# More of the U part ahead of the dense loop, gathers opened later, gates on ScalarE: one change to a streaming-encoder block

## The chip, the cores and the metric

The kernel runs on one core of a Trainium2 chip. A core has five engines that run on their own queues: TensorE (PE, with its weight loads PEld), VectorE (DVE), ScalarE (ACT), GpSimd (POOL) and SyncE (SP, which here only issues DMAs). The metric is the device time of one execution in microseconds (us); smaller is better.

## The reference

One encoder layer on 1024 tokens of width 1024. Two kinds of attention (stick-breaking and mLSTM) are mixed by an output projection; then a PEER mixer picks, for every token, 8 heads x 16 experts out of 16,384 and adds their outputs. The PEER part, cut to what matters here:

```python
scores = einsum('bshpc,hpnc->bshpn', h @ w_q, sub_keys)       # two halves of 128 keys per head
top_s, top_i = top_k(scores, 16)                              # then the best 16 of 16 x 16 sums
gate = softmax(best_s)                                        # 128 (expert, gate) pairs per token
u = expert_u[idx]; act = gelu(einsum('td,tkd->tk', x, u))     # U part
y = einsum('tk,tkd->td', gate * act, expert_v[idx])           # V part
```

All is float32. The kernel splits an operand into a rounded high half and a low half (high = round(x), low = x - high) and multiplies three pairs of halves.

## The kernel before

The 1024 tokens are cut into a group of 512 and two of 256. The PEER mixer treats them in two ways.

**Gathers.** 448 tokens (`G`) fetch their experts' rows: for each of 3 full tiles of 128 tokens, and a half tile that is packed onto 128 partitions, an indirect DMA on GpSimd's queue fetches one row of U per token (`gu`, 512 KB), VectorE multiplies it with the token and sums (L920); after all experts of the tile, another set of indirect DMAs fetches rows of V (`gv`), which VectorE scales and adds into `gy` (L931). That makes 448 + 448 = 896 gathers, in one stream, with four buffers (`GU`). The pool `gp` holds those buffers.

**Dense.** The other 576 tokens (`ND`) multiply with all 16,384 experts, in 128 blocks of 128 experts. The U part of a block (`block`) loads 512 KB of U, splits it (`uh` on ScalarE, `ul` on VectorE), makes 48 matmuls `da` and a gelu on ScalarE into `dg`. The V part (`dense`, `dense_out`) multiplies `dg` with a table of gates `dw`, splits it and a block of V, and makes 48 matmuls: 24 (`yr`) stay in PSUM all the time, 24 (`dy`) are summed there over `GB` blocks, then copied by ScalarE to `dt` and added to `dy` by VectorE.

**Gate table.** `wbuild` turns the experts and gates of 128 tokens into the table `w_d` in DRAM. It works in units of four tokens, 144 in all. A unit makes two one-hot tables, `wo1` from the first key (L985) and `o2` from the second (L986), on VectorE, scales the first with the gates on GpSimd into `wm` (L988), multiplies them per token on TensorE (`wps`), and ScalarE copies the result into `wst` (L993). In two of eight units (`ACT_HOT`) ScalarE makes the scaled second table instead (L981, L982) and VectorE only `wm` (L978). 32 tokens fill a `wst`, which goes to DRAM in one store of 2 MB; there are 18.

**Order.** The program is written as generators that `weave` mixes by their weights; a scheduler then orders each engine's instructions by priority (`urgent` raises it) and by when operands and buffers are there. The rough course: projections and the first attention part; attention for the later tokens beside `route(0)` and `route(1)` (the top-k of the first two groups); `out_proj(2)` and the first builds; `route(2)` beside more builds, U parts ahead (`ahead`, blocks of the list `AHEAD`, results kept in `g_d`) and the first gathers; the last builds; the dense loop with the rest of the gathers. `N_A` says how many blocks ahead, `N_G` how many gathers are mixed into these last two stages before the loop.

## Time and profile before

| | us |
|---|---|
| median of 3 runs | 3553.79 |
| lowest, highest | 3552.81, 3560.16 |
| the profiled execution's own time | 3561.83 |
| span of the profiled execution, first to last instruction | 3560.1 |

The profile is one execution. Over the span PE is busy 3048.9 us (86%), DVE 2954.9 (83%), ACT 1505.4 (42%), POOL 2024.9 (57%); the mean granted TensorE clock is 0.914 of 2.4 GHz. Since the limits change along the span, it is read by stretches: in a table of stretches each row has the stretch's bounds and length, then for every engine its busy time and count of instructions, then the granted clock, the mean busy share of the 16 DMA engines, and GB/s. A busy PE is not PE at its peak, since matmuls overlap.

### The profile page before, as it was taken

Reading aid. Unit: us, or ns where it says so; the run is one execution under the profiler, and the core shown is the slowest. Engines: PE = TensorE matmul, PEld = TensorE weight load, DVE = VectorE, ACT = ScalarE, POOL = GpSimd, SP = SyncE. Lnnn points to the kernel's source line nnn. Section 1 sums busy time; section 2 is a strip of 40 time slices with the busy share of each in tenths; the row PEclk is TensorE's granted clock in tenths of the full one; section 3 lists DMA queues with packets and bytes.
Section 4 is the critical chain, followed back from the end, with each engine's and each line's share of the span. In section 5 each row is a group of like instructions: output and inputs, shape, how many; then the busy total and the mean of one; then the engine's idle time right before and its main releaser. Section 6 shows DMA issues by size and latency. Waiting matters only on the chain.

```text
span 3560.1 us, 53635 instructions
## 1 busy us (share of the span) xinstructions
PE 3048.9 (86%) x18453; PEld 2738.0 (77%) x18453; DVE 2954.9 (83%) x5535; ACT 1505.4 (42%) x3195; POOL 2024.9 (57%) x1769
## 2 busy tenths in 40 slices
PE   6899998888877477975969999999999999999980
PEld 4677675566655367865969999999999999999980
DVE  6687745599999999998878888788888888888886
ACT  4665567845754335422543333333333333333320
POOL 4544445455888786675654455445555555555555
PEclk8999998899977678987979999999999999999995
DMA  4234426422466676677779998898999999998987
GB/s 171 82 118 132 121 68 199 142 86 79 134 212 192 200 238 223 212 234 258 245 267 323 314 313 306 297 324 303 331 317 318 311 319 319 329 332 312 326 274 270
DMA packets 403378, 850.16 MB, mean 239 GB/s; under 512 B 39320, under 2 KB 225176, under 8 KB 400800
## 3 DMA queue, kind: packets, MB, share of 16 engines
q0 software_dynamic: 129024, 469.82, 38.5%
q1 hardware_dynamic: 264480, 370.61, 31.8%
q10 hardware_dynamic: 9600, 6.29, 0.6%
q8 instruction: 145, 2.38, 0.3%
q14 instruction: 129, 1.06, 0.1%
HBM read 775.35 MB, written 70.95 MB: 238 GB/s over the span
## 4 chain that ended last, share of the span: by engine, by line
DVE 28%; PE 22%; issue 17%; DMA 16%; POOL 10%; ACT 2%; SPq 0%; POOLq 0%; DVEq 0%; ACTq 0%
DMA gv<-in_V_dram,idx 8%; POOL gu L918 7%; DVE gy L931 4%; DVE gu L920 3%; POOL gv L929 3%; DMA gu<-in_U_dram,idx 2%; PE wps L992 2%; DMA vf<-in_V_dram 2%; PE da L129 2%; PE da L131 2%; PE da L130 2%; DVE wo L986 2%; DVE wo L985 2%; PE dy L130 1%; PE dy L131 1%
## 5 line engine op out<-in xcount | busy, mean ns | idle before, releaser
L929 POOL DMA_INDIRECT gv<-in_V_dram,idx x384 | 504.7, 1314 | 438.3 <-DVE gy L931 361.2
L918 POOL DMA_INDIRECT gu<-in_U_dram,idx x384 | 498.6, 1298 | 424.8 <-DVE gu L920 355.1
L931 DVE SCALAR_TENSOR_TENSOR gy<-gv,gA,gy 128x1024 f32<-128x1024 f32 x448 | 595.7, 1330 | 121.1 <-DMA gv<-in_V_dram,idx 114.5
L920 DVE SCALAR_TENSOR_TENSOR gu<-gu,gh 128x1024 f32<-128x1024 f32 x448 | 582.4, 1308 | 117.6 <-DMA gu<-in_U_dram,idx 111.8
L131 PE MATMUL da<-dah,ul 128*128 128x320 f32 x1024 | 326.5, 319 | 41.0 <-DVE ul L125 40.9
L129 PE MATMUL da<-dah,uh 128*128 128x320 f32 x1024 | 326.6, 319 | 17.8 <-ACT dg L946 8.7
L1075 ACT COPY dt<-dy 128x320 f32<-128x320 f32 x336 | 142.4, 426 | 467.9 <-PE dy L131 362.5
L992 PE MATMUL wps<-wm,wo 128*128 128x128 f32 x1152 | 278.8, 408 | 57.7 <-DVE wo L986 39.9
L130 PE MATMUL da<-dal,uh 128*128 128x320 f32 x1024 | 324.4, 317 | 0.0
L129 PE MATMUL dy<-dgh,vh 128*128 128x320 f32 x1024 | 317.1, 312 | 4.4 <-ACT dt L1075 4.2
L131 PE MATMUL dy<-dgh,vl 128*128 128x320 f32 x1024 | 318.3, 311 | 0.0
L130 PE MATMUL dy<-dgl,vh 128*128 128x320 f32 x1024 | 318.2, 311 | 0.0
L129 PE MATMUL yr<-dgh,vh 128*128 128x256 f32 x1024 | 286.5, 285 | 27.9 <-ACT dgh L121 24.9
L129 PE MATMUL da<-h2h,uh 128*128 128x256 f32 x1024 | 290.2, 283 | 12.8 <-ACT dg L946 12.8
L992 PEld LDWEIGHTS wps<-wm,wo 128*128 128x128 f32 x1152 | 239.3, 233 | 79.3 <-issue 31.8
L130 PE MATMUL yr<-dgl,vh 128*128 128x256 f32 x1024 | 290.5, 285 | 3.4 <-DVE dgl L125 3.4
L131 PE MATMUL yr<-dgh,vl 128*128 128x256 f32 x1024 | 290.0, 284 | 0.5 <-DVE vl L125 0.5
L130 PE MATMUL da<-h2l,uh 128*128 128x256 f32 x1024 | 289.0, 282 | 0.0
L131 PE MATMUL da<-h2h,ul 128*128 128x256 f32 x1024 | 288.1, 281 | 0.0
L131 PEld LDWEIGHTS da<-dah,ul 128*128 128x128 f32 x1024 | 199.6, 195 | 44.8 <-DVE ul L125 44.3
L129 PEld LDWEIGHTS yr<-dgh,vh 128*128 128x128 f32 x1024 | 194.4, 192 | 29.1 <-ACT dgh L121 25.8
L129 PEld LDWEIGHTS da<-dah,uh 128*128 128x128 f32 x1024 | 200.2, 195 | 19.6 <-ACT dg L946 9.1
(450 smaller groups left out, 9155.4 us busy)
## 6 DMA issues: line engine op xcount, KB each, us to landing
uf<-in_UT_dram SPq DMA_DIRECT2D x128, 512.0 KB
vf<-in_V_dram SPq DMA_DIRECT2D x128, 512.0 KB
w_d<-wst SPq DMA_DIRECT2D x18, 2048.0 KB
dw<-w_d SPq DMA_DIRECT2D x32, 1152.0 KB
wfwq<-in_w_q_dram SPq DMA_DIRECT2D x192, 128.0 KB
wada<-in_w_adaT_dram SPq DMA_DIRECT2D x64, 256.0 KB
wfwo<-in_w_out_dram SPq DMA_DIRECT2D x96, 128.0 KB
wada<-in_w_adaT_dram SPq DMA_DIRECT2D x16, 512.0 KB
```

The costliest lines, as they stand in the source:

```text
L129: mm(out, sh, mh, start=start, stop=False, skip_group_check=skip)
L130: mm(out, sh, ml, start=False, stop=False, skip_group_check=skip)
L131: mm(out, sl, mh, start=False, stop=stop, skip_group_check=skip)
L918: nc.gpsimd.indirect_dma_start(out=u, out_offset=None, in_=a["U"], in_offset=bass.IndirectOffsetOnAxis(ap=idx[:, k : k + 1], axis=0))
L920: nc.vector.scalar_tensor_tensor(out=u, in0=u, scalar=1.0, in1=h2, op0=ALU.mult, op1=ALU.mult, accum_out=A[:, k : k + 1])
L929: nc.gpsimd.indirect_dma_start(out=vv, out_offset=None, in_=a["V"], in_offset=bass.IndirectOffsetOnAxis(ap=idx[:, k : k + 1], axis=0))
L931: nc.vector.scalar_tensor_tensor(out=y, in0=vv, scalar=A[:, k : k + 1], in1=y, op0=ALU.mult, op1=ALU.add)
L985: nc.vector.tensor_tensor(out=o1, **hot1)
L986: nc.vector.tensor_tensor(out=o2, in0=self.iota.unsqueeze(1).to_broadcast([P, 4, P]), in1=i2g[:, 0, ts].unsqueeze(2).to_broadcast([P, 4, P ...
L992: nc.tensor.matmul(ps[:, t], o2[:, t], m[:, :, t], start=True, stop=True)
L1075: nc.scalar.copy(t, ps)
```

## The change

- `AHEAD` grows from 12 blocks to 34; `N_A` from (6, 6) to (12, 22). The first 12 use the old single-buffered pool, the others the dense loop's own pool `ua`. `N_G` goes from (64, 64) to (96, 96).
- The gather pool `gp` is opened behind the attention pools, beside `mxp`, instead of ahead of `route(1)`.
- The stage that holds the end of `route(1)` and `out_proj(2)` gives the raised priority to the projection alone.
- In `wbuild` four ScalarE activations with a per-token scale replace GpSimd's product; `m` is laid out per token; `ACT_HOT` keeps one unit of eight instead of two.
- `GB` is 4 instead of 3: `dy` is summed over four blocks in PSUM.
- The last of the 18 gate groups gets DRAM tiles of its own (`we_d`, three stores for blocks 0-3, 4-31, 32-127), and the table for the first four blocks is asked for ahead of that group's build (`w_first`).
- In the first part of the kernel low halves move from GpSimd to VectorE and high halves from VectorE to ScalarE; weights there are loaded and split in 2 pieces instead of 4. `mod_q` moves to another pool.

```diff
+LAST = ((0, BB), (BB, 32), (32, 128))
-ACT_HOT = 5 * [(3, 7)]
+ACT_HOT = 5 * [(7,)]
-GB = 3
+GB = 4
-N_A = (6, 6)
+N_A = (12, 22)
-AHEAD = [3, 4, 5, 6, 7, 9, 11, 13, 15, 17, 19, 21]
+AHEAD = [4, 5, 6, 7] + list(range(10, 128, 4))
-N_G = (64, 64)
+N_G = (96, 96)
...
-        for q in range(4):
-            ks = slice(2 * q, 2 * q + 2)
-            wf = w.tile([P, 2, 128], F32, tag="wf", name=f"wf{name}_{q}", bufs=3)
+        n, e = (4, "v") if w is self.wp else (2, "g")
+        for q in range(KB // n):
+            ks = slice(n * q, n * q + n)
+            wf = w.tile([P, n, 128], F32, tag="wf", name=f"wf{name}_{q}", bufs=3)
             self.nc.sync.dma_start(wf, src[:, ks])
-            self.split(wf, wh[:, ks], wl[:, ks], "s", "g")
+            self.split(wf, wh[:, ks], wl[:, ks], "s", e)
...
-        self.split(L, Lh, Ll, "s" if on else "v", "g")
+        self.split(L, Lh, Ll, "s", "g" if on else "v")
...
-            self.split(W, *parts, "v", "g")
+            self.split(W, *parts)
...
-            self.split(Pm[:, live], ph[:, live], pl[:, live], "s" if f else "v", "g")
+            self.split(Pm[:, live], ph[:, live], pl[:, live], "s", "g" if f else "v")
...
+            if i == NG - 1:
+                self.w_first = self.gates_of(0)
...
-                    nc.gpsimd.tensor_tensor(out=m, in0=o1, in1=i2g[:, 1, ts].unsqueeze(1).to_broadcast([P, P, 4]),
-                                            op=ALU.mult)
+                    m = wb.tile([P, 4, P], F32, tag="wm", name=f"wm_{nm}", bufs=4)
+                    for t in range(4):
+                        col = slice(ts.start + t, ts.start + t + 1)
+                        nc.scalar.activation(m[:, t], o1[:, :, t], AF.Copy, scale=i2g[:, 1, col])
+                    ms = [m[:, t] for t in range(4)]
...
-            nc.sync.dma_start(self.w_d[i], st)
+            if i < NG - 1:
+                nc.sync.dma_start(self.w_d[i], st)
+            else:
+                for (b0, b1), w in zip(LAST, self.we_d):
+                    nc.sync.dma_start(w, st[:, b0:b1])
...
-                wt = self.wr.tile([P, NG, BB, TB], F32, tag="dw", name=f"dw{b}", bufs=2)
-                nc.sync.dma_start(wt, self.w_d[:, :, b : b + BB].rearrange("g i b t -> i g b t"))
+                wt = self.gates_of(b) if b else self.w_first
+                b0, w = next((b0, w) for (b0, b1), w in zip(LAST, self.we_d) if b0 <= b < b1)
+                (nc.sync if b else nc.gpsimd).dma_start(wt[:, NG - 1], w[:, b - b0 : b - b0 + BB])
...
-                self.gp = enter(left("gp"))
-                gathers = self.gathers()
...
-            self.mxp = enter(left("mxp"))
+            self.mxp, self.gp = enter(left("mxp")), enter(left("gp"))
+            gathers = self.gathers()
...
-            run(woven((first(r), 10 * (24 - CUT[3])), (first(chain(upto(p), upto(p))), 95), (wbs(*W_T[0]), 1.8 * 32 * len(W_T[0]))))
+            run(woven((r, 10 * (24 - CUT[3])), (first(chain(upto(p), upto(p))), 95), (wbs(*W_T[0]), 1.8 * 32 * len(W_T[0]))))
...
-                for b in AHEAD:
-                    nc.sync.dma_start(self.g_d[b], self.block(b, ub, (1, 1)))
+                for x, b in enumerate(AHEAD):
+                    nc.sync.dma_start(self.g_d[b], self.block(b, ub, (1, 1)) if x < N_A[0] else self.block(b, ua))
```

The order of instructions shows the change at three places. In the names, the last number is a tile's own; the one ahead of it counts (`gu_0` is the first gathered row of a tile of tokens). The first place is VectorE where the first gather stands. Before, it is amid the attention of the last tokens (`L`, `dm`) and the norm of the second group (`h`, `dal`):

```order
L505 SCALAR_TENSOR_TENSOR L_768_4_10603<-zs_768_4_10602,L_768_4_10603 128x512
L307 SCALAR_TENSOR_TENSOR dal<-h_3_9856,mod,dah 128x256
L920 SCALAR_TENSOR_TENSOR gu_0_13081,gA_13080<-gu_0_13081,gh_3_13071 128x1024
L723 SCALAR_TENSOR_TENSOR h_4_9887<-h_4_9887,scol_141,rwyh_9763 128x256
L505 SCALAR_TENSOR_TENSOR L_768_3_10713<-zs_768_3_10712,L_768_3_10713 128x512
L920 SCALAR_TENSOR_TENSOR gu_1_13096,gA_13080<-gu_1_13096,gh_3_13071 128x1024
```

Now it is amid the builds of the first gate tile (`wo`) and the last top-k of `route(1)`:

```order
L993 TENSOR_TENSOR wo_0_3_2_12495<-iota,wi_0_12137 128x512
L992 TENSOR_TENSOR wo_0_3_3_12561<-iota_b,wi_0_12135 128x512
L924 SCALAR_TENSOR_TENSOR gu_0_13000,gA_12999<-gu_0_13000,gh_3_12990 128x1024
L993 TENSOR_TENSOR wo_0_3_3_12560<-iota,wi_0_12137 128x512
L815 MAX gate<-mr_6_0_11951 128x8
L924 SCALAR_TENSOR_TENSOR gu_1_13003,gA_12999<-gu_1_13003,gh_3_12990 128x1024
```

The stream of gathers thus begins behind the attention, where 21 one-hot tables are already made.

The second place is TensorE at the last build unit. Before, units follow one another and the V part (`yr`, `dy`) follows at once:

```order
L992 MATMUL wps_3_6_17047<-wm_3_6_17042,wo_4_3_6_17041 128x128 x4
L992 MATMUL wps_3_7_17067<-wm_3_7_17057,wo_4_3_7_17056 128x128 x4
L129 MATMUL yr_17082<-dgh_17155,vh_17148 128x256
L129 MATMUL yr_17083<-dgh_17155,vh_17148 128x256
L129 MATMUL yr_17084<-dgh_17155,vh_17148 128x256
```

Now the unit's matmuls stand between those of U blocks (`da`), of which 473 follow before the first of the V part:

```order
L1002 MATMUL wps_3_7_18766<-wm_3_7_18756,wo_4_3_7_18755 128x128 x2
L131 MATMUL da_0_17843<-dah,uh_17839 128x320
L132 MATMUL da_0_17843<-dal,uh_17839 128x320
L133 MATMUL da_0_17843<-dah,ul_17840 128x320
L1002 MATMUL wps_3_7_18766<-wm_3_7_18756,wo_4_3_7_18755 128x128
```

Between the last matmul of the routing and the first of the V part there are 1221 U matmuls now and 504 before; 36 blocks' U matmuls stand ahead of the V part instead of 16.

The third place is VectorE at the end of the dense loop (`dy<-dy,dt` are its last adds, `dx` the output of the dense tokens). Before, the last tile's V gathers have come to their 89th of 128:

```order
L931 SCALAR_TENSOR_TENSOR gy_32196<-gv_88_34328,gA_29025,gy_32196 128x1024
L1048 SCALAR_TENSOR_TENSOR dx_3_35295<-yr_17083,mod,dx_3_35295 128x256
L1076 TENSOR_TENSOR dy<-dy,dt_35246 128x320
L1076 TENSOR_TENSOR dy<-dy,dt_35259 128x320
L931 SCALAR_TENSOR_TENSOR gy_32196<-gv_89_34401,gA_29025,gy_32196 128x1024
```

Now that tile's U gathers have come to their 124th:

```order
L924 SCALAR_TENSOR_TENSOR gu_123_32170,gA_29183<-gu_123_32170,gh_2_29181 128x1024
L1069 SCALAR_TENSOR_TENSOR dx_3_35215<-dy,mod,dx_3_35215 128x320
L1097 TENSOR_TENSOR dy<-dy,dt_35145 128x320
L1097 TENSOR_TENSOR dy<-dy,dt_35164 128x320
L924 SCALAR_TENSOR_TENSOR gu_124_32173,gA_29183<-gu_124_32173,gh_2_29181 128x1024
```

Behind the last add stand 132 gathers instead of 40.

## Rows read from the trace of the kernel before

**Rows 1.** The page's first line.

```profile
span 3560.1 us, 53635 instructions
```

**Rows 2.** Table of stretches, all instructions: PE, PEld, DVE, ACT, POOL, clock, DMA.

```profile
0.00:560.00 560.00, 481.57 (x2002) 356.56 (x2002) 372.67 (x657) 337.70 (x692) 248.20 (x253) 0.93 0.39 118
560.00:1000.00 440.00, 391.61 (x1735) 282.81 (x1735) 353.62 (x1310) 289.51 (x741) 269.29 (x315) 0.92 0.42 126
1000.00:1214.00 214.00, 131.24 (x624) 97.93 (x624) 209.79 (x636) 82.64 (x208) 179.03 (x158) 0.76 0.69 216
1214.00:1600.00 386.00, 298.99 (x1622) 278.18 (x1622) 375.33 (x749) 161.19 (x395) 276.22 (x241) 0.82 0.66 220
1600.00:1852.00 252.00, 186.34 (x950) 173.51 (x950) 219.30 (x347) 100.84 (x225) 159.49 (x122) 0.84 0.73 253
1852.00:3468.00 1616.00, 1559.15 (x11520) 1548.97 (x11520) 1365.80 (x1791) 533.49 (x937) 846.05 (x647) 0.99 0.91 315
3468.00:3560.00 92.00, 0.00 (x0) 0.00 (x0) 58.39 (x53) 0.00 (x0) 46.61 (x37) 0.50 0.79 275
```

**Rows 3.** Stretches, tiles gu, gu, gv alone: DVE, POOL (x126: two per gather).

```profile
1000.00:1214.00 214.00, 96.04 (x126) 75.66 (x60) 0.76 0.69 216
1214.00:1600.00 386.00, 17.79 (x27) 19.55 (x16) 0.82 0.66 220
1214.00:1600.00 386.00, 103.90 (x64) 73.48 (x61) 0.82 0.66 220
```

**Rows 4.** Groups by line and shape: count | busy us, mean ns | idle before, its releasers.

```profile
L986 DVE TENSOR_TENSOR wo<-iota,wi 128x512 f32<-128x512 f32 x108 | 107.0, 1005 | 3.8 <-PE wps L992 3.8
L985 DVE TENSOR_TENSOR wo<-iota_b,wi 128x512 bf16<-128x512 bf16 x108 | 89.3, 844 | 0.0
L978 DVE TENSOR_TENSOR wm<-iota_b,wi 128x512 f32<-128x512 bf16 x36 | 35.3, 981 | 2.3 <-PE wps L992 2.1
L988 POOL TENSOR_TENSOR wm<-wo,wi 128x512 f32<-128x512 bf16 x108 | 134.7, 1257 | 57.7 <-PE wps L992 30.3 <-DVE wi L964 7.5 <-issue 6.0
L982 ACT ACTIVATE wo<-wo,wi,wi 128x128 f32<-128x128 f32 x144 | 62.2, 488 | 0.0
L981 ACT ACTIVATE wo<-iota,wi 128x128 f32<-128x128 f32 x144 | 47.2, 394 | 45.2 <-DVE wi L966 26.9 <-PE wps L992 18.3
L993 ACT COPY wst<-wps 128x512 f32<-128x512 f32 x144 | 83.0, 581 | 116.4 <-PE wps L992 114.0 <-issue 1.7
```

**Rows 5.** Timeline, from 1308 us: start, length, instruction [idle before it].

```profile
1308.18 3.22 DVE L986 TENSOR_TENSOR wo<-iota,wi 128x512 f32<-128x512 f32 x1
1308.80 2.04 POOL L988 TENSOR_TENSOR wm<-wo,wi 128x512 f32<-128x512 bf16 x2
1311.32 0.41 DVE L985 TENSOR_TENSOR wo<-iota_b,wi 128x512 bf16<-128x512 bf16 x1
...
1311.66 0.68 DVE L986 TENSOR_TENSOR wo<-iota,wi 128x512 f32<-128x512 f32 x1
```

**Rows 6.** Stretches: tile da alone (PE, PEld, ACT), then all instructions.

```profile
1600.00:1852.00 252.00, 77.65 (x432) 69.13 (x432) 6.92 (x17) 0.84 0.73 253
3000.00:3200.00 200.00, 196.94 (x1478) 195.97 (x1477) 171.34 (x273) 66.87 (x117) 106.13 (x84) 1.00 0.94 327
```

**Rows 7.** Groups by line and shape: the adds and copies of the dense loop.

```profile
L1076 DVE TENSOR_TENSOR dy<-dy,dt 128x320 f32<-128x320 f32 x336 | 160.0, 484 | 15.2 <-ACT dt L1075 13.2 <-issue 1.5
L1075 ACT COPY dt<-dy 128x320 f32<-128x320 f32 x336 | 142.4, 426 | 467.9 <-PE dy L131 362.5 <-DVE dy L1076 92.6 <-PE da L131 4.0
```

**Rows 8.** Groups by line and shape, POOL, 0 to 560 us.

```profile
L125 POOL TENSOR_TENSOR Wl<-W,Wh 128x512 fp32r<-128x512 f32 x16 | 22.7, 1418 | 10.0 <-DVE Wh L123 10.0
```

**Rows 9.** The end: stretches, tile gv alone (DVE, POOL); waits from 3468 us.

```profile
3490.20:3553.80 63.60, 41.14 (x32) 36.00 (x28) 0.50 0.81 273
3468.00:3553.80 85.80, 51.39 (x40) 46.61 (x37) 0.50 0.84 288
DVE gy L931 <- DMA gv<-in_V_dram,idx: 26.4, 28, 3.1
```

More of the change, by code (lines that the diff above doesn't have):

```diff
@@ L203, in consts @@
         self.mod = c.tile([P, 48], F32, name="mod")
-        self.mod_q = c.tile([P, 2, 48], F32, name="mod_q")
+        self.mod_q = e.tile([P, 2, 48], F32, name="mod_q")
         self.scol = e.tile([P, KB], F32, name="scol")
@@ L331, in keep @@
         if not f:
-            self.split(src, parts[0], parts[1], "s", "g")
+            self.split(src, parts[0], parts[1])
     def proj_sb(self, p):
@@ L371, in proj_v @@
             if not f:
-                self.split(t, v[0], v[1], "s", "g")
+                self.split(t, v[0], v[1])
             yield
@@ L973, in wbuild @@
                 o2 = wb.tile([P, 4, P], F32, tag="wo2", name=f"wo2_{nm}", bufs=4)
-                m = wb.tile([P, P, 4], F32, tag="wm", name=f"wm_{nm}", bufs=4)
                 hot1 = dict(in0=self.iota_b, in1=i1[:, ts].unsqueeze(1).to_broadcast([P, P, 4]), op=ALU.is_equal)
                 if q % 8 in ACT_HOT[T]:
+                    m = wb.tile([P, P, 4], F32, tag="wm", name=f"wm_{nm}", bufs=4)
                     nc.vector.tensor_tensor(out=m, **hot1)
+                    ms = [m[:, :, t] for t in range(4)]
                     for t in range(4):
@@ L987, in wbuild @@
                                             in1=i2g[:, 0, ts].unsqueeze(2).to_broadcast([P, 4, P]), op=ALU.is_equal)
-                    nc.gpsimd.tensor_tensor(out=m, in0=o1, in1=i2g[:, 1, ts].unsqueeze(1).to_broadcast([P, P, 4]),
-                                            op=ALU.mult)
+                    m = wb.tile([P, 4, P], F32, tag="wm", name=f"wm_{nm}", bufs=4)
[3 more added lines that the diff above has]
+                    ms = [m[:, t] for t in range(4)]
                 ps = pp.tile([P, 4, P], F32, tag=tags[q % 2], name=f"wps{nm}")
                 for t in range(4):
-                    nc.tensor.matmul(ps[:, t], o2[:, t], m[:, :, t], start=True, stop=True)
+                    nc.tensor.matmul(ps[:, t], o2[:, t], ms[t], start=True, stop=True)
                 nc.scalar.copy(st[:, :, 4 * q : 4 * q + 4], ps.rearrange("p t n -> p n t"))
                 yield 1.8
-            nc.sync.dma_start(self.w_d[i], st)
+            if i < NG - 1:
[3 more added lines that the diff above has]
+                    nc.sync.dma_start(w, st[:, b0:b1])
     def block(self, b, ua, bufs=(DG, 2)):
@@ L1014, in block, with gates_of @@
         return g
+    def gates_of(self, b):
+        wt = self.wr.tile([P, NG, BB, TB], F32, tag="dw", name=f"dw{b}", bufs=2)
+        self.nc.sync.dma_start(wt[:, 0 : NG - 1], self.w_d[:, :, b : b + BB].rearrange("g i b t -> i g b t"))
+        return wt
     def dense(self, ua, dn):
@@ L1093, in build @@
         self.g_d = tiles("g_d", max(AHEAD) + 1, [P, ND])
-        self.w_d = dr.tile([NG, P, NB, TB], F32, name="w_d")
+        self.w_d = dr.tile([NG - 1, P, NB, TB], F32, name="w_d")
+        self.we_d = [dr.tile([P, b1 - b0, TB], F32, name=f"we_d{b0}") for b0, b1 in LAST]
         self.pp = pool("ps", 2, space=bass.MemoryType.PSUM)
```

## The prediction

> **What bounds the kernel now.** The table of stretches [rows 2] cuts the span of 3560.1 us [rows 1] at places that can be found in the trace: the end of the first attention part (560), the first gather (about 1000), the first gate build (1214), the end of the last routing (1600), the first matmul of the V part (1852) and its last add (3468). To 1000 TensorE is busy 482 of 560 and 392 of 440. From 1000 to 1600 VectorE is: 210 of 214 and 375 of 386, TensorE only 131 and 299. From 1600 to 1852 both have holes (186 and 219 of 252). In the dense loop TensorE has 1559 of 1616, 11,520 matmuls. The last 92 us hold no matmul, only gathers, for whose landings VectorE waits [rows 9]. So three limits follow each other, and the end of the kernel is the end of the gather stream. An edit is worth what it does to the limit of its stretch.
>
> **The change part by part.** Times of the order of work are counts of rows of the two orders; durations are rows of the trace.
>
> *0 to 560.* 112 subtractions of weight halves leave GpSimd and become 56 twice as wide on VectorE; 88 low halves of keys, scores and products follow; 64 high halves go from VectorE to ScalarE. A 128x512 low half took 1.42 us on GpSimd [rows 8]; VectorE does a two-operand 128x512 in 0.68 when it is not held up [rows 5]. By that, VectorE gains about 144 instructions, some 88 us, loses 64 casts of the same widths (by estimate no dearer than the subtractions) and the hold-ups by GpSimd's tensor work, which was most of its 248 us: near even on an engine with 373 of 560. TensorE is the limit here, and its idle time, 78 us, is the most there is to win; the shorter chains of split, product, split give part of it. I take -8, between -40 and +10 (the next stretch has VectorE at 80% and TensorE at 89%, more than here, so a busier VectorE costs little).
>
> *1000 to 1214.* The gather pool now opens behind the attention, so the first gather stands behind the first builds in VectorE's order instead of amid the attention. All 63 gathers of this stretch leave it: VectorE 96.0 us [rows 3] out of 210. What then ends last? TensorE's 131 us, at a granted clock of 0.76; with the idle share of the stretch before (11%) that is 147 us, -67, and less if the clock rises to the 0.92 of that stretch. Between -60 and -96; I take -78, nearer to TensorE's limit. The projection set ahead of the routing changes the order within, and neither's amount.
>
> *1214 to 1600.* 80 build units stand here before and after. A unit was two one-hot products on VectorE, 1.005 and 0.844 us on average, and a gate product of 1.26 us on GpSimd [rows 4]. The timeline shows why the average is high: an L986 took 3.22 us with GpSimd's gate products inside it, and 0.68 without; an L985 took 0.41 [rows 5]. With the gates on ScalarE (4 x 0.394, the rows of 128x128 activations [rows 4]), 70 units cost VectorE 1.09 each and 10 cost 0.68, together 83 us; before, 60 x 1.85 plus 20 x 0.98 were 131. That is -48, and other instructions that the gate products held up give some more, -8. Against it stand 105 gathers instead of 77 [rows 3], 28 x 1.29 (41.14 for 32 where nothing holds them up [rows 9]) = +36, and 5 more U blocks' 128x1024 splits at the same 1.29, +6. That is -14; with what the fewer hold-ups give the gathers (1.62 each here, 103.90 for 64 [rows 3]) I take -20, from -45 to +15. GpSimd's gate products took 134.7 us in all, and the means exceed the free durations by 108 x (0.33 + 0.43) = 82 us.
>
> The Trainium skill, "SBUF — State Buffer", section "Who interferes with whom", says that a VectorE instruction with two inputs in SBUF and a GpSimd instruction that reads SBUF shut each other out for the whole instruction, and that ScalarE waits on no one. By that rule the whole 134.7 us would come back to VectorE; the row of averages bears out 82 of it, and I use the rows. By the rule the sum would be lower by about 50 us, if VectorE always had work.
>
> *1600 to 1852.* 64 units before and after, but TensorE's order has 1221 U matmuls between the routing's last and the V part's first, against 504: 717 more, at 0.140 us (1616 over 11,520 [rows 2]) 100 us. 186 + 100 = 286 us, and at the dense loop's share of 96.5% 297: +45. TensorE then is the limit. Its clock was 0.84 here and would be near the loop's 0.99 with its holes filled; that takes some 5 us off. I take +40, from +20 to +75. VectorE (219, less the hold-ups by 48 gate products, plus 13 splits and 9 gathers) stays below, and the blocks' stores and loads are some 7 MB on DMA engines that are at 0.73. ScalarE gains 504 x 0.394 = 199 us over the two build stretches, loses 72 x (0.394 + 0.488) = 64, and gains some 1.9 for each of 20 U blocks (two gelus of 0.41, 6.92 for 17 [rows 6], and a 128x1024 cast, by estimate twice the 0.58 of a 128x512 copy [rows 4]): 262 becomes some 435 of about 660. Cover enough, unless its waits grow (below).
>
> *The dense loop.* 36 blocks' U part lies ahead of it instead of 16, so 10,560 matmuls are left. At the loop's mean of 0.140 that is 1481 us, at that of its best 200 us, 200 over 1478 [rows 6], 1429. The gathers inside are fewer (580 against 645 in VectorE's order), and V in fours takes away 88 adds of 0.48 us and 88 copies of 0.43 [rows 7], about 80 us on engines that TensorE sometimes waits for. I take 0.138: 1457, so -159, between -125 and -187. The gates' last group in three stores, and its extra small loads, lie beside this.
>
> *The end.* In VectorE's order 132 gathers now stand behind the last add of the dense loop; before it was 40. The 40 took 85.8 us and the last 32 of them 63.6, 1.99 each [rows 9]. 92 more cost 92 x 1.99 = +183. With 1.9 each it is +175; at the pace inside the loop, 1616 over 645 = 2.5, +230.
>
> **The sum:** -8 - 78 - 20 + 40 - 159 + 183 = -42, so a span of 3518 and, with 1.7 us around it, 3520. The profiled execution took 3561.83, 8 us more than the median of 3553.79; I take 8 off: **3512 us**. Most of what TensorE gains it hands to a longer gather tail, because the gathers start some 140 us later and the loop around them shrinks.
>
> **Rivals.** *ScalarE paces the builds* (slower). A unit's four scalings stand in one queue with the copy of the unit before, which waits for TensorE. 4 x 0.394 + 0.58 is 2.2 us per unit, 144 units 311 us, beside U blocks. For it: ScalarE already waited 116 us in front of that copy [rows 4], and now each wait holds the next unit's gates too. Against it: 435 of 660 leaves room, and buffers are four deep. Price: 1214 to 1600 becomes +40 and 1600 to 1852 +75 instead of -20 and +40, 95 us more: 3607. It decides from 42 us on, that is when the two build stretches together last over 700 us instead of 658.
>
> *TensorE closes its holes* (faster). The loop runs at its best pace (-187) and the builds' end costs +20, since the clock rises; the tail at 1.9. 3512 - 28 - 20 - 8 = 3456. For it: the pace of 0.135 is seen over whole stretches; against it: DMA engines at 0.91 in the loop.
>
> *The terms cancel* (no change): a loop at its old mean (-135 instead of -159) and a tail at 2.1 each (+193 instead of +183) are enough: 3546. The change does do what it says: the order has 36 split U blocks ahead of the first gate product of the loop, against 18.
>
> **How the numbers follow.** The forecast, 3480 to 3546, 0.48; TensorE closing its holes, 0.18; no change, 0.11; ScalarE pacing, or a tail as slow as in the loop, 0.23. Faster by over 0.2% is 0.66, same 0.11, slower 0.23 (0.2% is about what a measurement of this kernel can tell from no change). The range takes in the ends of the large terms, tail and loop, and most of both outer cases: 3450 to 3600.
>
> **What would show it.** Right: the first gather near 1140; stretches with builds where L986 and L985 take 0.68 and 0.41 throughout; the first V matmul near 1785; its last add near 3245; then some 270 us without a matmul, at 2 us per gather. Wrong: ScalarE idle in front of the copy of a build unit while TensorE waits for a scaled gate; a first V matmul after 1830; a loop above 1480; a tail above 300 or below 250.

## The result, and the profile after

The changed kernel took 3511.37 us (median; 3502.86 to 3513.13) beside 3555.35 for the kernel before: ratio 0.987, interval 0.985 to 0.989, 44 us faster. The forecast was 3512.

The profiled execution's span stands against [rows 1]:

```profile
span 3511.4 us, 53484 instructions
```

The limits change at events, and the events moved, so the stretches are cut here at the events of each kernel: the first top-k of the routing, the first gate unit, the last top-k, the first V matmul, the last add into `dy`, the end. Columns as in [rows 2]: bounds, length, busy time of PE, PEld, DVE, ACT, POOL, clock, DMA share, GB/s. First after:

```profile
0.00:697.90 697.90, 614.30 (x2582) 448.80 (x2583) 446.53 (x882) 476.31 (x991) 119.90 (x155) 0.94 0.42 131
697.90:1120.20 422.30, 365.79 (x1805) 275.05 (x1803) 395.87 (x1669) 251.93 (x659) 260.76 (x305) 0.92 0.32 98
1120.20:1517.20 397.00, 288.55 (x1838) 271.33 (x1838) 362.59 (x895) 218.55 (x605) 258.97 (x217) 0.82 0.79 269
1517.20:1786.70 269.50, 223.87 (x1671) 220.55 (x1672) 203.89 (x324) 168.94 (x432) 102.30 (x81) 0.91 0.88 314
1786.70:3249.90 1463.20, 1420.02 (x10562) 1413.36 (x10560) 1223.79 (x1633) 463.24 (x784) 766.80 (x579) 0.99 0.92 319
3249.90:3511.00 261.10, 0.00 (x0) 0.00 (x0) 174.97 (x148) 0.31 (x1) 152.81 (x128) 0.50 0.82 274
```

The same table of the kernel before, at the same events:

```profile
0.00:709.60 709.60, 617.75 (x2581) 452.20 (x2582) 452.84 (x801) 455.68 (x983) 334.01 (x355) 0.93 0.42 129
709.60:1218.00 508.40, 389.56 (x1794) 288.00 (x1794) 487.23 (x1817) 256.32 (x659) 362.50 (x371) 0.85 0.50 152
1218.00:1617.00 399.00, 305.09 (x1663) 283.65 (x1661) 385.17 (x790) 163.26 (x398) 285.40 (x248) 0.82 0.66 221
1617.00:1853.50 236.50, 177.34 (x898) 165.14 (x898) 206.96 (x292) 97.33 (x221) 151.81 (x115) 0.84 0.72 252
1853.50:3468.30 1614.80, 1559.15 (x11520) 1548.97 (x11520) 1364.60 (x1787) 532.78 (x936) 844.85 (x647) 0.99 0.91 315
3468.30:3560.00 91.70, 0.00 (x0) 0.00 (x0) 58.09 (x53) 0.00 (x0) 46.31 (x37) 0.50 0.79 274
```

Row by row, after less before, with the forecast term in brackets: -12 (-8), -86 (-78), -2 (-20), +33 (+40), -152 (-159), +170 (+183). The sum is -49 (-42). (The forecast's stretches were cut at slightly other places, so a term and its row agree only to some us.) Three of the six rows are large, and they largely cancel: the last add comes 218 us earlier (3250 instead of 3468), and 170 of that is handed to a stretch without a matmul.

The units' instructions, groups by line (count, busy us, mean ns, idle before and its releaser), against [rows 4]; L992 and L993 are the one-hot products of L985 and L986, L998 the new scalings, L1003 the copy:

```profile
L993 DVE TENSOR_TENSOR wo<-iota,wi 128x512 f32<-128x512 f32 x126 | 89.8, 728 | 5.0 <-PE wps L1002 4.9
L992 DVE TENSOR_TENSOR wo<-iota_b,wi 128x512 bf16<-128x512 bf16 x126 | 61.0, 498 | 2.9 <-ACT wm L998 2.9
L998 ACT ACTIVATE wm<-wo,wi 128x128 f32<-128x128 bf16 x504 | 165.7, 406 | 51.5 <-DVE wo L992 50.8 <-DVE wi L968 0.7
L1003 ACT COPY wst<-wps 128x512 f32<-128x512 f32 x144 | 82.5, 576 | 18.4 <-PE wps L1002 18.1
```

VectorE's two products fell from 1.005 and 0.844 us to 0.73 and 0.50. ScalarE's wait in front of the copy fell from 116 us to 18, and the new scalings wait for VectorE (51 us) far more than VectorE waits for them (3 us).

The gate matmuls on TensorE changed too. No term of the forecast has this. They are two instructions per token; first before, then after:

```profile
L992 PE MATMUL wps<-wm,wo 128*128 128x128 f32 x1152 | 278.8, 408 | 57.7 <-DVE wo L986 39.9 <-DVE wm L978 10.8 <-POOL wm L988 3.5
L1002 PE MATMUL wps<-wm,wo 128*128 128x128 f32 x1152 | 186.0, 314 | 42.1 <-DVE wo L993 16.5 <-ACT wm L998 13.6 <-DVE wm L984 4.8
```

They keep TensorE busy 93 us less. It goes with the layout: the scalings write `wm` per token, so that a matmul reads neighbouring elements, where it read every fourth one before. The changed kernel shows both layouts side by side. From 1600 to 1717 us, at a granted clock of 1.00, it runs 360 instructions of this group. In the 48 that follow VectorE's six `wm` of that time (the units of `ACT_HOT`, still in the old layout) one took 0.38 to 0.40 us, as all took before; nearly all others took 0.28.

### The profile page after: what moved, and what is told of

It reads as the page before. It is cut to its first block, busy times and chain, and to the rows that moved or that the text cites. A ratio compares the mean times of both kernels' runs of the same rounds, so it can differ in the third digit from the quotient of the medians.

```text
span 3511.4 us, 53484 instructions
## 1 busy us (share of the span) xinstructions
PE 2912.5 (83%) x18453; PEld 2629.1 (75%) x18453; DVE 2807.7 (80%) x5545; ACT 1579.3 (45%) x3471; POOL 1661.5 (47%) x1462
## 4 chain that ended last, share of the span: by engine, by line
PE 26%; DMA 19%; issue 19%; DVE 18%; POOL 14%; ACT 3%; SPq 0%; POOLq 0%; DVEq 0%; ACTq 0%
DMA gv<-in_V_dram,idx 11%; POOL gu L922 9%; POOL gv L933 4%; DVE gy L935 3%; PE da L131 2%; PE da L133 2%; PE da L132 2%; DMA gu<-in_U_dram,idx 2%; PE wps L1002 2%; DMA gu<-in_U_dram,gix 1%; PE z L496 1%; DVE gu L924 1%; DMA vf<-in_V_dram 1%; DMA wada<-in_w_adaT_dram 1%; PE ipc L131 1%
## 5 line engine op out<-in xcount | busy, mean ns | idle before, releaser
L935 DVE SCALAR_TENSOR_TENSOR gy<-gv,gA,gy 128x1024 f32<-128x1024 f32 x448 | 583.3, 1302 | 168.9 <-DMA gv<-in_V_dram,idx 159.0
L933 POOL DMA_INDIRECT gv<-in_V_dram,idx x384 | 492.5, 1283 | 411.9 <-DVE gy L935 319.7
L924 DVE SCALAR_TENSOR_TENSOR gu<-gu,gh 128x1024 f32<-128x1024 f32 x448 | 555.2, 1249 | 148.3 <-DMA gu<-in_U_dram,idx 127.5
L1096 ACT COPY dt<-dy 128x320 f32<-128x320 f32 x248 | 105.7, 427 | 476.2 <-PE dy L133 399.4
L127 POOL TENSOR_TENSOR vlm<-kvrm,vhm 128x128 fp32r<-128x128 f32 x56 | 29.5, 528 | 451.6 <-ACT vhm L123 446.9
L1002 PE MATMUL wps<-wm,wo 128*128 128x128 f32 x1152 | 186.0, 314 | 42.1 <-DVE wo L993 16.5
L1002 PEld LDWEIGHTS wps<-wm,wo 128*128 128x128 f32 x1152 | 169.4, 216 | 49.1 <-ACT wm L998 31.5
```

The source lines that it names most:

```text
L127: e.tensor_sub(lo, src, hi.bitcast(F32))
L924: nc.vector.scalar_tensor_tensor(out=u, in0=u, scalar=1.0, in1=h2, op0=ALU.mult, op1=ALU.mult, accum_out=A[:, k : k + 1])
L933: nc.gpsimd.indirect_dma_start(out=vv, out_offset=None, in_=a["V"], in_offset=bass.IndirectOffsetOnAxis(ap=idx[:, k : k + 1], axis=0))
L935: nc.vector.scalar_tensor_tensor(out=y, in0=vv, scalar=A[:, k : k + 1], in1=y, op0=ALU.mult, op1=ALU.add)
L1002: nc.tensor.matmul(ps[:, t], o2[:, t], ms[t], start=True, stop=True)
L1096: nc.scalar.copy(t, ps)
```

## The experiments

Runs are numbered 1 to 12 in the order in which they stand here. Ratios are to the kernel before on the same chip, and their intervals are 95%. Runs 1 to 4, 5 to 7, 8 to 10 and 11 to 12 had a chip each, on which the kernel before took 3547 to 3556 us, so a difference of medians between these groups can be off by some 8 us. Lengths of stretches are those between the events above, each from one profiled execution.

**1. Which parts pay: the first four runs.** The gather pool early again:

```diff
-            self.mxp, self.gp = enter(left("mxp")), enter(left("gp"))
-            gathers = self.gathers()
+            self.mxp = enter(left("mxp"))
 ...
+                self.gp = enter(left("gp"))
+                gathers = self.gathers()
                 r = chain(self.early(xw), p, route(1))
```

> The changed kernel with the gather pool opened where it was before, ahead of the second half of the attention; all else as changed. In VectorE's order 63 gathers now stand ahead of the first gate build (0 in the changed kernel), and 67 behind the last add of the dense loop (132). Theory (each gather is paid once, at the pace of the place where it stands): the first gate build comes 80 to 98 us later (63 gathers at 1.53 us of VectorE), the tail gets 65 x 1.9 = 124 us shorter: 3511 + 88 - 124 = 3475 us. So the late opening would be a loss inside a winning change. Rival 1, the late opening is a gain of its own, since TensorE idles longer amid the gathers than VectorE works on them: the first build comes 98 us later, the tail is only 65 x 1.3 = 85 us shorter: 3524 or more. Rival 2, both are even: 3500 to 3511.

Measured: 3461.29 us, ratio 0.9746 (0.9715 to 0.9778). The table of stretches of this run, from the first top-k to the end:

```profile
700.90:1207.80 506.90, 386.09 (x1791) 285.75 (x1790) 488.12 (x1815) 254.99 (x658) 362.08 (x371) 0.85 0.50 152
1207.80:1600.50 392.70, 286.74 (x1854) 267.37 (x1852) 366.82 (x856) 223.15 (x610) 272.65 (x211) 0.85 0.78 263
1600.50:1882.70 282.20, 233.33 (x1743) 229.60 (x1744) 214.03 (x366) 173.48 (x440) 111.41 (x93) 0.91 0.90 323
1882.70:3324.00 1441.30, 1408.70 (x10489) 1403.73 (x10488) 1207.94 (x1545) 458.40 (x776) 750.29 (x568) 0.99 0.92 319
3324.00:3471.00 147.00, 0.00 (x0) 0.00 (x0) 98.01 (x86) 0.85 (x2) 74.56 (x66) 0.51 0.81 277
```

The first gate unit comes 88 us later, and the end without matmuls is 121 us shorter (148 against 269 from the last matmul, 63 gathers fewer). The stretches between make -6 together: the loop is shorter, the builds' end longer. So the theory holds (3475 us expected; this profiled execution took 3473, the longest of the four): a gather that stands early costs 88/63 = 1.4 us, one that is left for the end 121/63 = 1.9. The late opening looks like a gain of 86 us in the table after, and is a loss of some 1.3% in the kernel.

The gate product back on GpSimd (and `ACT_HOT` as before):

```diff
-                    for t in range(4):
-                        col = slice(ts.start + t, ts.start + t + 1)
-                        nc.scalar.activation(m[:, t], o1[:, :, t], AF.Copy, scale=i2g[:, 1, col])
+                    nc.gpsimd.tensor_tensor(out=m, in0=o1, in1=i2g[:, 1, ts].unsqueeze(1).to_broadcast([P, P, 4]),
+                                            op=ALU.mult)
```

> The changed kernel with the gate product back on GpSimd, and the quarter of the units with ScalarE's one-hot as before. 92 gathers stand ahead of the end of the last routing (105), 147 behind the last add (132). Theory (GpSimd's gate products hold VectorE's two-operand work up): VectorE's mean for the one-hot products goes back from 0.73 and 0.50 us to about 1.0 and 0.85; the stretch from the first build to the end of the routing gets 56 us longer less 13 x 1.29 for the gathers that left it, +39; the tail gets 15 x 1.9 = 28 us longer: 3511 + 67 = 3578 us. Rival, ScalarE paces the builds in the changed kernel as much as VectorE did before (the stretch is 397 us there against 399): the stretch keeps its length, 3511 + 28 - 17 = 3522 us.

Measured: 3586.95 us, ratio 1.012 (1.008 to 1.016), slower than the kernel before. Groups by line:

```profile
L996 POOL TENSOR_TENSOR wm<-wo,wi 128x512 f32<-128x512 bf16 x108 | 140.5, 1309 | 62.1 <-PE wps L1001 51.3 <-DVE gy L935 3.2 <-DVE wo L992 2.9
L993 DVE TENSOR_TENSOR wo<-iota,wi 128x512 f32<-128x512 f32 x108 | 106.7, 1002 | 13.1 <-PE wps L1001 13.1
L992 DVE TENSOR_TENSOR wo<-iota_b,wi 128x512 bf16<-128x512 bf16 x108 | 74.2, 703 | 4.7 <-POOL wm L996 4.7
```

With GpSimd's products the means of VectorE's two are 1.00 us, back where it was, and 0.70, between 0.50 and the 0.844 of before. The loss is 75 us by the medians (2.5% by the ratios), near the theory's 67, but it lies elsewhere. The stretch of builds and routing is 415 us (397), +18 where the theory had +39; the next is 312 (269), +43 where it had nothing; the loop is some 12 shorter, and the end behind the last matmul 297 (269), +28 as expected. The two middle stretches of this run, and its gate matmuls:

```profile
1115.70:1530.80 415.10, 327.76 (x1838) 305.14 (x1838) 400.87 (x874) 164.64 (x405) 322.11 (x264) 0.85 0.71 240
1530.80:1843.00 312.20, 271.46 (x1671) 259.67 (x1672) 234.72 (x297) 129.64 (x272) 171.09 (x126) 0.93 0.77 268
L1001 PE MATMUL wps<-wm,wo 128*128 128x128 f32 x1152 | 286.2, 405 | 39.3 <-DVE wo L993 20.9 <-POOL wm L996 10.3 <-DVE wm L984 6.1
```

VectorE is the limit of the first, at 401 of 415. In the second TensorE is: from 1600 us to its end it is busy 241 of 243 us, at a granted clock of 1.00. It runs the same 1671 matmuls there in 271 us instead of 224, and the gate matmuls alone, in their old layout again, take 52 us more. So the +43 are TensorE's, and the layout's. The edit takes back two things at once, GpSimd's rest and the layout. No run has one without the other. The rival, ScalarE as the pace, is out: its time fell, and the kernel got slower.

The list of 12 early blocks (`N_A` and `N_G` as before):

```diff
-AHEAD = [4, 5, 6, 7] + list(range(10, 128, 4))
+AHEAD = [3, 4, 5, 6, 7, 9, 11, 13, 15, 17, 19, 21]
```

> The changed kernel with the list of 12 blocks early, and the counts of before for how they and the gathers are woven; all else as changed. 76 gathers stand behind the last add (132). Theory (the loop's gain is handed to the tail): the loop gets some 22 blocks x 48 matmuls x 0.138 = 146 us longer, the stretch between the routing's end and the first V matmul some 33 to 40 us shorter, and the tail 56 x 1.9 = 106 us shorter: 3511 + 146 - 37 - 106 = 3514 us, the same within 10. Rival, the early blocks are the change's main gain (TensorE's holes at the builds' end get filled): the tail does not shrink by as much, 60 to 110 us slower, 3570 to 3620.

Measured: 3481.66 us, ratio 0.9817 (0.9795 to 0.9838), where the theory had 3514: faster than with 34 blocks, by 30 us in the medians, 40 in the profiled runs and 0.5% in the ratios. Its stretches from the first gate unit:

```profile
1114.00:1493.90 379.90, 259.93 (x1550) 237.69 (x1550) 346.79 (x880) 208.35 (x587) 251.88 (x211) 0.79 0.77 260
1493.90:1722.80 228.90, 138.51 (x998) 135.14 (x998) 173.65 (x283) 143.51 (x389) 93.17 (x69) 0.78 0.81 284
1722.80:3307.50 1584.70, 1551.20 (x11520) 1545.07 (x11520) 1333.27 (x1740) 502.64 (x845) 861.53 (x650) 0.99 0.92 320
3307.50:3471.00 163.50, 0.00 (x0) 0.00 (x0) 109.50 (x95) 0.85 (x2) 87.14 (x75) 0.51 0.82 279
```

The loop is 129 us longer than with 34, the builds' end 41 shorter, the tail 105 shorter (163.7 against 269 from the last matmul): +129 - 41 - 105 = -17. The theory's three terms were +146, -37 and -106. Another 17 us were in no theory: the stretch of builds and routing is 380 us instead of 397. VectorE is busy 16 us less in it; 8 of these are the splits of the six U blocks, and some 3 the five gathers, that no longer stand there. The first gate unit comes 6 us earlier besides. TensorE's holes are back (138.5 busy of 229) and nothing is lost by that.

The kernel before with ScalarE's gates and nothing else (their per-token layout and `ACT_HOT` with one unit of eight belong to them):

> The kernel before with nothing changed but the gate product: four scalings on ScalarE instead of one product on GpSimd, and one unit in eight with ScalarE's one-hot instead of two. 160 gathers stand ahead of the end of the last routing (141), 7 behind the last add (40). Theory: the stretch from the first build to the end of the routing gets 56 us shorter, less 19 more gathers at 1.29, so -31; the stretch behind it up to 10 us shorter; the tail 33 x 1.9 = 63 us shorter: 3554 - 31 - 63 - 5 = 3455 us, faster than the changed kernel. Rival, ScalarE paces the builds: the stretch stays at 399 us or grows, 3554 - 63 + 0 to 40: 3490 to 3530 us. Rival 2, the gathers inside the loop (654 against 645) and the missing tail make the loop itself longer, by 33 x 1.9: 3520.

Measured: 3441.16 us, ratio 0.9708 (0.9675 to 0.9741): more than twice the gain of the whole change, and 14 us below the theory. Three groups, and the stretches from the first gate unit:

```profile
L987 DVE TENSOR_TENSOR wo<-iota,wi 128x512 f32<-128x512 f32 x126 | 92.0, 746 | 1.7 <-PE wps L996 1.7
L986 DVE TENSOR_TENSOR wo<-iota_b,wi 128x512 bf16<-128x512 bf16 x126 | 55.1, 451 | 0.0
L996 PE MATMUL wps<-wm,wo 128*128 128x128 f32 x1152 | 184.2, 316 | 58.6 <-DVE wo L987 27.9 <-ACT wm L992 13.7 <-DVE wm L978 8.8
```

```profile
1210.30:1586.30 376.00, 267.39 (x1658) 248.80 (x1657) 346.27 (x840) 214.39 (x596) 261.45 (x208) 0.82 0.78 263
1586.30:1806.50 220.20, 138.21 (x903) 131.59 (x903) 179.76 (x328) 140.65 (x384) 99.20 (x82) 0.81 0.86 308
1806.50:3412.00 1605.50, 1556.75 (x11520) 1546.33 (x11520) 1364.59 (x1749) 529.76 (x935) 859.77 (x644) 0.99 0.92 315
3412.00:3441.00 29.00, 0.00 (x0) 0.00 (x0) 17.69 (x23) 0.67 (x2) 6.05 (x5) 0.56 0.78 278
```

Builds and routing 376 us instead of 399, the stretch behind 220 instead of 236, and 65 us less from the last matmul to the end (29 against 94, 8 gathers against 41); with 8 us ahead of the first unit and 7 in the loop, 119 in the profiled runs. In builds and routing VectorE, at 385 of 399 us before, is busy 346 although 21 more gathers stand in the stretch. VectorE's freed time was filled with gathers, and these are what shortened the end. TensorE's busy time fell as well, by the new layout (from 305 to 267 and from 177 to 138 in the two stretches); what that adds where VectorE is the limit was not separated.

**2. Both losses taken back, fours against threes, and the tail.** The pool early and 12 blocks early together:

> The changed kernel with both parts taken back that the last runs showed to cost time: the gather pool opened where it was before, and the list of 12 early blocks. What is left of the change is the gates on ScalarE, the splits of the attention that went from GpSimd to VectorE and ScalarE, the last projection ahead of the routing, and V in fours. 63 gathers stand ahead of the first build, 6 behind the last add. Theory (the two losses add up, and what is left beside the gates is worth some 10 us): 3461 - 30 + 6 for the tail that can't shrink below nothing = 3437 us, as the kernel before with ScalarE's gates alone (3441) or up to 15 us less. Rival, the splits and the projection are worth as much as the front showed in the changed kernel (10 us earlier at the first routing): 3410 to 3425. Rival 2, they cost: 3450 or more.

Measured: 3439.25 us, ratio 0.9695 (0.9659 to 0.9732). The two losses add up, and what is left beside ScalarE's gates is nothing that can be told from run 4. The projection ahead of the routing, one of these parts, was never run alone.

The same in threes:

```diff
-GB = 4
+GB = 3
```

> The run of both parts taken back, and V in threes as before. 88 adds of 0.48 us on VectorE and 88 copies of 0.43 on ScalarE come back into the dense loop. No tail of gathers is left to take it up (7 behind the last add). Theory (TensorE waits now and then for these engines, loop at 0.140 instead of 0.138 per matmul): 10 to 20 us slower than with fours. Rival, the loop is paced by the bytes that its DMA moves and fours change nothing: within 5 us.

Measured: 3471.07 us, ratio 0.9778 (0.9746 to 0.9809): 32 us slower by the medians, 0.8% of the kernel before, above the theory's 10 to 20. In the profiled executions it is 24 us, 14 of them from the first V matmul to the last (1623 against 1609).

Six gather buffers for the V gathers of the last tile (threes make the room):

```diff
+            if T == NH - 1 and k % 3 == 2:
+                vv = self.dn.tile([P, D], F32, tag="gx", name=f"gv{T}_{k}", bufs=2)
+            else:
+                vv = g.tile([P, D], F32, tag="gu", name=f"gv{T}_{k}", bufs=GU)
```

> The changed kernel with V in threes, which leaves room in the dense loop's pool for two more gather buffers, and with these two used by the V gathers of the last tile alone (every third of them), so that six gathers are in flight there instead of four. 129 gathers stand behind the last add (132). What is read is the pace of the tail: 1.9 us per gather in the changed kernel, with DMA engines at 0.84 and VectorE waiting 78 us for landings in 255 us. Theory (the tail is paced by what the DMA engines move): 1.75 to 1.9 per gather, tail 225 to 255 us. Rival, it is paced by the round trip through four buffers (GpSimd waits 64 us there for VectorE to give one back): 1.35 to 1.5 per gather, VectorE's own 1.3, tail 175 to 195 us, and the kernel some 70 us faster.

Measured: 3480.24 us, ratio 0.9797 (0.9759 to 0.9834), of two executions. Its partner is run 11 below, the same in threes with four buffers, 3534.82. The end without matmuls is 218 us instead of 270, for 131 and 132 gathers. What is waited for in this end, in run 11 (engine, what it waits for, us in total, times, longest):

```profile
DVE gy L935 <- DMA gv<-in_V_dram,idx: 82.0, 95, 2.4
POOL gv L933 <- DVE gy L935: 55.2, 55, 2.1
```

and with six buffers:

```profile
DVE gy L938 <- DMA gv<-in_V_dram,idx: 29.4, 53, 2.7
POOL gv L936 <- DVE gy L938: 4.1, 3, 1.7
```

A stretch of 200 us in this end, V gathers alone (DVE, POOL, clock, DMA share, GB/s), first of the changed kernel (run 11 issues 104 in the same 200 us too), then with six buffers:

```profile
3300.00:3500.00 200.00, 133.60 (x104) 123.90 (x104) 0.50 0.83 274
```

```profile
3270.00:3470.00 200.00, 163.15 (x127) 151.56 (x123) 0.50 0.94 342
```

GpSimd hardly waits any more for VectorE to give a buffer back, and the pace goes from 1.92 us per gather (200 over 104) to 1.57 (200 over 127), between the ranges of theory and rival. That the round trip through four buffers held the tail up is shown. What paces it at six is not: the DMA engines at 0.94 are the fullest (VectorE has 163 of 200 us, GpSimd 152), but no run has more buffers.

**3. What is left of the change.** The kernel before with ScalarE's gates and V in fours:

> The kernel before with the gates on ScalarE and, new here, V in fours (a small table of the modulation moves to a pool that closes early, to make room). Nothing else of the change is in it. 4 gathers stand behind the last add. Theory (fours are worth what the pair of runs in fours and threes showed, 0.8%, about 28 us, since the end of the dense loop is now the end of the kernel): 3441 - 28 = 3413 us. It would then be the fastest, and the other parts of the change (splits, projection, last group of gates in three stores) would cost some 25 us between them. Rival, fours only win back in the changed kernel what its extra loads cost there: 3430 to 3445 us.

Measured: 3447.76 us, ratio 0.9692 (0.9651 to 0.9734): no gain over run 4, where the theory had 28 us. The gates' last group stored whole again, on run 5:

> The run with both losses taken back (pool early, 12 early blocks, V in fours), and the gates' last group stored whole and loaded with the others as before: 31 small loads of 64 KB fewer in the dense loop. Theory (they lie beside other work, as the prediction had it): 3439 us, the same within 8. Rival, the small loads hold up the gate product of every fourth block (ScalarE's dgh split waits 248 us for it in the loop, and TensorE 32 us for that split): 15 to 25 us faster, 3414 to 3424.

Measured: 3434.02 us, ratio 0.9649 (0.9609 to 0.9689). The intervals of runs 5 and 9 overlap, and the loop has the same length (1610 and 1609 us), so the small loads don't hold it up. It is the fastest version of all, by its median, though not clear of run 5. The splits of the attention back on GpSimd, on run 5:

```diff
 ...
-            self.split(src, parts[0], parts[1])
+            self.split(src, parts[0], parts[1], "s", "g")
 ...
-            self.split(W, *parts)
+            self.split(W, *parts, "v", "g")
 ...
```

> The run with both losses taken back, and the splits of the attention's weights, keys, scores and products where they were before, on GpSimd, with the high halves as before. 3 gathers stand behind the last add (6). Theory (VectorE is far from full to 560 us and TensorE sets the end there; the first routing began 12 us earlier in the changed kernel): the first routing begins 8 to 12 us later, and the end with it: 3447 to 3451 us. Rival, the wider splits give TensorE nothing that lasts to the end, or cost by the work they put on VectorE to 1200 us: 3425 to 3439.

Measured: 3443.53 us, ratio 0.9684 (0.9639 to 0.9728). In the profile the first top-k comes at 702 us instead of 692, and the last add some 13 us later, as the theory had it; the medians differ by 4 us, inside their intervals. Over all profiles the first top-k comes at 702 to 710 us in the four kernels with the old splits and at 692 to 701 in the ten with the new ones. So the splits bring TensorE's first part forward by some 10 us, and what of that reaches the end can't be told.

The changed kernel in threes:

> The changed kernel with V in threes as before, nothing else. 130 gathers stand behind the last add (132). The two pairs so far disagree: fours were worth 28 us where the pool was early and 12 blocks were early, and nothing on the kernel before with ScalarE's gates. Theory (as the prediction had it, loop at 0.140 instead of 0.1385 per matmul): the loop gets 10,560 x 0.0015 = 16 us longer, 2 gathers fewer are left for the tail, the end comes 12 us later: 3523. Rival, ScalarE's dt copies that TensorE waits for (5 us in the loop) are all that fours touch: within 5 us of 3511. Rival 2, as in the pair that showed it: 3536 or more.

Measured: 3534.82 us, ratio 0.9967 (0.9944 to 0.999). In the changed kernel fours are worth 1.0%. The loop of this run, and what TensorE waits for in it:

```profile
1789.40:3264.40 1475.00, 1417.82 (x10489) 1407.74 (x10487) 1245.51 (x1702) 491.01 (x865) 755.47 (x573) 0.99 0.91 314
```

```profile
PE yr L131 <- ACT dgh L123: 28.9, 20, 5.5
PE yr L132 <- DVE dgl L127: 17.4, 10, 4.3
```

In the changed kernel these two are 1.8 and 2.7 us, and the wait for the U part's gelu is 25.4:

```profile
PE da L131 <- ACT dg L950: 25.4, 16, 4.5
PE yr L132 <- DVE dgl L127: 2.7, 3, 1.9
PE yr L131 <- ACT dgh L123: 1.8, 1, 1.8
```

From the first V matmul to the last it is 19 us longer (1475 against 1456), although 72 U matmuls fewer stand in it: 0.1406 us per matmul instead of 0.1379, or 28 us at the same count, where the theory had 16. It begins 3 us later, and the tail does not get shorter by what the loop gets longer. That makes the 23 us of the medians, near rival 2 and not the theory. Why fours bring nothing on the kernel before with ScalarE's gates (run 8) stays open: there TensorE waits as long in fours as in threes (74 and 72 us in the loop), and the loop is as long (1609 and 1605 us).

20 blocks early instead of 12, on run 9:

> The run with the pool early, the gates whole, V in fours, and 20 blocks early instead of 12. 38 gathers stand behind the last add (10). Theory (with 12 there is hardly a tail left, so the end is set by the stream of gathers and loads; a block early adds 0.59 MB of store and load, 8 of them 4.7 MB, 15 us at 316 GB/s, and gives only TensorE something): loop 8 x 48 x 0.14 = 54 us shorter, builds' end 10 to 20 longer, tail 28 x 1.9 = 53 longer: 3434 + 15 = 3449 us. Rival, the 80 us in which TensorE is idle between the routing's end and the first V matmul are filled by them at no cost: 3400 to 3420 us.

Measured: 3447.18 us, ratio 0.9704 (0.9674 to 0.9734). The stretches from the last top-k, with the first one of run 9 ahead of them:

```profile
1570.00:1788.80 218.80, 134.51 (x998) 130.38 (x998) 182.05 (x327) 142.08 (x388) 94.20 (x80) 0.81 0.86 313
1581.70:1807.60 225.90, 169.62 (x1286) 167.22 (x1287) 185.27 (x328) 151.96 (x406) 96.21 (x77) 0.87 0.89 318
1807.60:3358.00 1550.40, 1502.63 (x11136) 1495.19 (x11136) 1288.95 (x1632) 488.70 (x823) 836.73 (x617) 0.99 0.92 317
3358.00:3445.00 87.00, 0.00 (x0) 0.00 (x0) 57.69 (x54) 0.43 (x1) 40.78 (x36) 0.53 0.82 282
```

TensorE's holes fill from 135 us busy of 219 to 170 of 226 and the loop gets 60 us shorter; the end behind the last matmul grows from 39 to 87, and the stretch of builds and routing by 14. No gain, as the theory had it. Whether it is the 0.59 MB per early block or VectorE's order of gathers that takes it away was not separated: by the page 34 early blocks move 13 MB more than 12 (the second line is run 3's):

```profile
DMA packets 402337, 863.13 MB, mean 246 GB/s; under 512 B 39672, under 2 KB 211192, under 8 KB 399760
```

```profile
DMA packets 395999, 850.13 MB, mean 245 GB/s; under 512 B 38968, under 2 KB 210488, under 8 KB 393424
```

At the loop's 319 GB/s that is 41 us, and the spans differ by 40. It fits, but no run moved the bytes alone.

## Why the prediction was right

*0 to the first routing*, -8: measured -12, and run 10 gives 10 of it to the splits. TensorE's idle time was the right place to look.

*To the first build*, -78: measured -86. The 63 gathers left, and the clock in the stretch rose from 0.85 to 0.92. That TensorE would be the limit there did not come out: VectorE is still the busier engine, 396 of 422 against 366. The value held because it was taken between the two bounds. The term is right as a stretch. The prediction did not set it against its own price in the tail; that was in its rows (63 x 1.53 of VectorE there, 63 x 1.99 at the end), and would have told that this part loses.

*Builds and routing*, -20: measured -2, the term with the largest miss. The hold-up by GpSimd was right in kind: VectorE's means rise with GpSimd's products (run 2) and fall without them (run 4). In the two one-hot products its size was 0.277 + 0.346 us per unit, 67 us over 108, where the forecast said 82; GpSimd's weight splits (`wlwq`, `wlwo`) still run beside the builds. VectorE's busy time did fall by what the forecast had added up, from 385 to 363 us. What failed is the step from there to the stretch, which was to shrink by as much. VectorE's idle time grew from 14 to 34 us. Waits for gathered rows to land are 17 of these 34 and were 8 before. Runs 3 and 4, with fewer U blocks in the stretch, leave VectorE as idle (33 and 30 us) but less busy (347 and 346). Why it waits more was not separated.

The rule of the Trainium skill quoted there ("SBUF — State Buffer", "Who interferes with whom"), by which all of GpSimd's 134.7 us would come back to VectorE, was too much for these two products by half: 67 us came back in them in the changed kernel and 70 in run 4. What VectorE's other instructions got back is not in that count. That ScalarE waits on no one fits the scalings' 0.41 us, beside 0.39 for ScalarE's like-sized activations.

*Builds' end*, +40: measured +33, by luck. The forecast added 100 us to TensorE's busy time and left it 3.5% idle. Its busy time rose by only 47 us (177 to 224), since the gate matmuls took 77 us there instead of 123 beside some 770 more U matmuls; and it is idle for 46 of the 269.5 us, 31 of them in one wait for the last top-k's result. The layout's gain and that wait, both missing from the forecast, offset each other. The clock rose to 0.91, not near 0.99; from 1600 us on, TensorE is the limit, as the forecast had it (117 of 117 us to 1717, at a granted clock of 1.00).

*Dense loop*, -159: measured -152. From first to last matmul it is 1456/10,560 = 0.1379 us (0.138). Without fours it is 1475/10,488 = 0.1406 in the changed kernel (run 11). Fours alone do not make this pace: runs 5 and 9 have them and more gathers in the loop, and show 0.140.

*Tail*, +183: measured +170, for 132 gathers as counted, at 1.92 us in its middle.

*The 8 us* that were taken off for the profiled execution of before: the last median of before is 3555.35, 6.5 below that execution, so most of this holds. But the profiled execution of the changed kernel is only 1.8 above its own median.

The mechanism was right where the large terms are: TensorE's gain in the loop, the gathers that leave the stretch ahead of the first build, and the tail they lengthen, each within 13 us. That the sum came out within 1 us of the median is luck: the six rows miss their terms by -4, -8, +18, -7, +7 and -13, the span by -7, and the 8 us taken off make up for it. The statement that TensorE's gain is handed to the tail is shown by run 3: the loop's 129 us and the tail's 105 go and come together. The rival that ScalarE paces the builds is refuted by runs 2 and 4. The signs came nearly as named: the two products at 0.73 and 0.50 us (0.68 and 0.41), the first gather at 1143 us, the first V matmul at 1787, the last add at 3250, then 269 us without a matmul. The sentence that fell short is the one that was missing: the change was summed by stretches, never by its parts. By parts it is ScalarE's gates (-3%), fours (-1% in this kernel), against the late pool (+1.3%) and 22 more early blocks (+0.5%). These do not add up to the -1.3% of the whole, since fours bring nothing on ScalarE's gates alone (run 8).

## What to carry to other kernels

Where a stream of transfers ends the kernel, price each part of a change to the end of that stream: work that is moved away from an early stretch comes back behind the last matmul, at that place's price per item. Look there first at how many buffers are in flight (four gave 1.92 us per gather, six 1.57). And take elementwise products off GpSimd where VectorE is the limit: what counts is not their own time, but that of VectorE's instructions beside them. Look also at what else such an edit changes: the layout that came with it halved the time from one of TensorE's gate matmuls to the next, and the forecast had no term for it.

## What was not expected of the hardware

- A tail of gathers at 0.83 DMA share and 274 GB/s was not at its limit: with six buffers instead of four the same engines showed 0.94 and 342 GB/s, while GpSimd's issue of one stayed at 1.2 us.
- The DMA share is not a rate: 319 GB/s at 0.92 in the dense loop are 347 per full share, 274 at 0.83 in the tail are 330, 342 at 0.94 are 364. So a share in one mix of transfers does not tell the rate in another.
- Without GpSimd's product on 128x512, VectorE's two products took 0.62 us less in all per unit, half of its own 1.26 us.
- A 128x128 float32 matmul that reads `wm` at every fourth element took 0.38 to 0.40 us and started 0.21 us after the one before it (medians). With neighbouring elements it took 0.28 and started 0.11 us after, in the same kernel at the same granted clock of 1.00.
